# A hybrid decoder block on one core: attention regrouped into rounds of four steps, with half-height score matmuls, half-width value matmuls and a combination by features

## The chip, the core and the metric

The kernel runs on one core of one Trainium2 chip. The core has a matmul engine (PE; its weight loads are listed apart as PEld), a vector engine (DVE), an activation engine (ACT), a general engine (POOL), a queue that issues most transfers (SP), and 16 DMA engines that all transfers share. The metric is device time in microseconds (us) of one execution; several executions are timed and the median is taken.

## What is computed

One decoder block over a sequence of 2048 positions of 1024 features, in float32. One input projection feeds two branches: attention (branch A) and a gated recurrence (branch B); their gated outputs are projected, merged, projected again and normalised. The change concerns branch A:

```python
DILATION_GROUPS = ((128, 1), (512, 4), (2048, 16))     # (window, dilation); 8 heads of 64 in each group
# per group: positions regrouped by residue modulo the dilation, blocks of 128 queries,
# keys = [previous block, current block], causal band of width window // dilation
s = jnp.einsum('brnqhd,brnkhd->brnhqk', qb, kw) * (Dh ** -0.5)
s = jnp.where(valid, s, NEG_INF)
m = jnp.max(s, -1); p = jnp.exp(s - m); l = jnp.sum(p, -1)
o = jnp.einsum('brnhqk,brnkhd->brnqhd', p, vw) / l
lse = m + jnp.log(l)
# over the groups, per head slot and position:
attn = sum_g softmax_g(lse_g) * o_g
attn = attn * silu(g_attn);  y_a = attn @ w_attn_proj
```

## The kernel before, in words

The program is one hand-written order of instructions for each engine. `now["n"]` counts ticks; `later(lag, fn)` puts `fn`'s instructions into the streams `lag` ticks on, and `pe_later` does the same for a place inside PE's stream. An engine executes its own stream strictly in that order, and SP issues its transfers in that order too: a transfer whose buffer is not free yet holds up those written behind it.

Four stages follow one another. (1) The input projection, seven-multiplication products of 512-column matmuls (line L598), with all elementwise work of both branches beside it; queries go to DRAM as a rounded part and a rest (`qh_scr`, `ql_scr`, both pre-scaled), keys as they are (`k_scr`), values transposed (`v_scr`). (2) Attention. (3) The recurrent branch's projection `yb` (L1198 to L1200), with the combination of the three groups beside it. (4) The attention projection `ya`, the output projection and the normalisation.

**Attention before.** There are 12 units: a unit is one dilation group g and one pair of heads `hp` (`unit(u)`, in the order of groups 0, 2, 1). A unit has 16 steps, one for each block of 128 queries, so there are 192 steps. A step has two key blocks of 128 where there is a previous block ("full", 108 steps), and one otherwise ("half": all 64 of group 2, four of each unit of group 1, one of each unit of group 0, together 84).

- `step_s` computes scores. Heads have 64 features, and the 128 rows of a matmul hold two things at once: `A` stacks the query's rounded part above its rest, `B1` (tile B) holds the key's rounded part twice, and `b2` (tile C) the key's rest above zeros. Two matmuls for each head, accumulated in one bank (L973), give the three products that float32 accuracy needs. DVE adds the mask and takes the row's extreme (`tensor_tensor_reduce`, L977, and a small read of its accumulator); ACT takes the exponential (L979).
- `step_t` transposes the probabilities on PE (L988, two for each head) and ACT or DVE brings them from PSUM to SBUF (L993, L995).
- `step_v` multiplies: the transposed probabilities `ptb` are the stationary operand, V the moving one with 65 columns, of which one is all ones and gives the denominator (L1012; each of these float32 matmuls is two instructions on PE). DVE copies two steps' outputs out (L1016), and ACT issues their transfer to `o_scr` (L1026), 132 floats for each position: values, denominators, extremes.

PE's stream takes turns: the scores of step m, the transposes of step m-3, the values of step m-4. A unit's operands are loaded one unit ahead by `unit_parts` (six transfers: L784, L805); POOL rounds and splits the keys (L792, L793, L795), three passes over each half of the rows. V is loaded for two units at a time (`v_parts`, L822 to L826). The slots X0 to X5 hold the projection's inputs until its last products have read them, so the first unit's loads wait for those.

**Combination before** (`combine`, 16 calls of 512 positions by one head pair): three loads of `o_scr` by position (positions on partitions), 17 small DVE operations and one exponential for the weights (L1114 to L1131), three POOL multiplications and two additions of 128x512 (L1133 to L1135), four PE transposes to features (L1140), and the gate on DVE (L1145).

Of the kernel before, what the change touches and what calls it, by code (L numbers as in the profile page):

```python
# [8 lines left out]
F32 = mybir.dt.float32  # L9
# [6 lines left out]
P = 128  # L16
# [15 lines left out]
def hybrid_block_kernel(ctx: ExitStack, tc: tile.TileContext, a: dict, out: bass.AP):  # L32
# [10 lines left out]
    o_scr = [[dram.tile([S, 132], F32, name=f"o_scr{g}{hp}") for hp in range(HP)] for g in range(3)]  # L43
# [5 lines left out]
    v_scr = [[dram.tile([S, 260], F32, name=f"v_scr{g}{j}") for j in range(2)] for g in range(3)]  # L49
# [286 lines left out]
    vs_free = [sl_p.tile([P, 4, 130], F32, name=f"vs{j}") for j in range(2)]  # L336
    for t in vs_free:
        dve.memset(t[:, :, 0:1], 1.0)
        dve.memset(t[:, :, 129:130], 1.0)
    tog = {"n": 0}  # L340

    def v_chain(vt, sgn, f, c):
# [14 lines left out]
        act.activation(vs[:, :, 1:129], st["tp"], AF.Copy, scale=sgn)  # L357
        tog["n"] -= 1
        yield Ask()
        dst = v_scr[g][hp // 2][c * CH:(c + 1) * CH, (hp % 2) * 130:(hp % 2) * 130 + 130]  # L360
# [395 lines left out]
    lo_, up_ = slice(0, 64), slice(64, P)  # L756
    USLOT = (("X4", "X3", "X2"), ("Y0", "X1", "X0"))
    VSLOT = {(0, 0): "X5", (2, 0): "Y1", (1, 0): "Y2", (0, 1): "X5", (2, 1): "Y1", (1, 1): "Y2"}
    zero = [False, False]
    B2 = {}  # L760
# [7 lines left out]
    def unit_parts(u):  # L768

        sl = USLOT[u % 2]  # L770
        g, hp = unit(u)
        q = {n: qk_scr[n, 4 * g + hp] for n in ("qh", "ql", "k")}

        def k_part(h, hs, os):
            def fn():
                if h == 0:
                    units[u] = [None, big(sl[1], [P, 2, S], F32R, f"B{u}")]
                    if u < 2:
                        B2[u] = big(sl[2], [P, 2, S], F32R, f"C{u}")
                        pool.memset(flat(B2[u][up_, 0]), 0.0)  # L780
                        pool.memset(flat(B2[u][lo_, 1]), 0.0)
                    units[u].append(B2[u % 2])
                _, B1, b2 = units[u]
                sp.dma_start(flat(b2[hs, h]), q["k"][hs])  # L784

                def split(t):
                    if (u, h) == (0, 0):
                        act.activation(B1[hs, h, t], flat(b2[hs, h, t]), AF.Copy)
                        act.activation(B1[os, h, t], flat(B1[hs, h, t]), AF.Copy)
                        eng = dve  # L790
                    else:
                        pool.tensor_copy(B1[hs, h, t], flat(b2[hs, h, t]))  # L792
                        pool.tensor_copy(B1[os, h, t], flat(B1[hs, h, t]))  # L793
                        eng = pool
                    eng.tensor_tensor(out=b2[hs, h, t], in0=flat(b2[hs, h, t]), in1=flat(B1[hs, h, t]), op=ALU.subtract)  # L795

                later(3, lambda: split(slice(0, S // 2)))
                later(4, lambda: split(slice(S // 2, S)))
            return fn

        def q_part(hs, h, n, qs):
            def fn():
                if (hs, h) == (lo_, 0):
                    units[u][0] = big(sl[0], [P, 2, S], F32R, f"A{u}")
                sp.dma_start(flat(units[u][0][hs, h]), q[n][qs])  # L805
            return fn

        return [k_part(0, lo_, up_), k_part(1, up_, lo_), q_part(lo_, 0, "qh", lo_), q_part(up_, 0, "ql", lo_),
                q_part(lo_, 1, "ql", up_), q_part(up_, 1, "qh", up_)]

    VT = {}

    def v_parts(g, j):
        src = v_scr[g][j]

        def part(i):
            def fn():
                if i == 0:
                    VT[g, j] = big(VSLOT[g, j], [P, 16, 260], F32, f"V{g}{j}")
# [82 lines left out]
    first, second, firstv = unit_parts(0), unit_parts(1), v_parts(0, 0)  # L902
    low = NS
    where = [(s, j) for s in range(NQ) for j in range(ticks[s])]
    for T, (s, j) in enumerate(where):
# [10 lines left out]
        if s == NQ - 1:  # L916
            for fn in ((), (), first[:2], first[2:], firstv, second[:1], second[1:2])[j]:
                fn()
# [32 lines left out]
    def step_s(m):  # L951
        u, n = divmod(m, 16)
        g, _ = unit(u)
        A, B1, b2 = units[u]
        pv = prev(g, n)
        lo = 0 if pv is not None else P
        s = aps.tile([P, 2, 256], F32, tag="s", name=f"s{m}", bufs=3)
        if n % 4 == 0:
            st["osb"] = at_p.tile([P, 4, 132], F32, tag="osb", name=f"osb{m}", bufs=6)
        osb = st["osb"]  # L960
        for h in range(2):
            q = A[:, h, n * P:(n + 1) * P]
            for i, B in enumerate((B1, b2)):
                if g == 2:
                    k = B[:, h].rearrange("p (c r i) -> p r c i", c=4, r=16)[:, max(n - 1, 0):n + 1]
                elif pv is None:
                    k = B[:, h, n * P:(n + 1) * P]
                elif g == 0:
                    k = B[:, h, (n - 1) * P:(n + 1) * P]
                else:  # L970
                    c, r = divmod(n, 4)
                    k = B[:, h, (c - 1) * CH:(c + 1) * CH].rearrange("p (c r j) -> p r c j", c=2, r=4)[:, r]
                pe.matmul(s[:, h, (0 if g == 2 and n else lo):256], q, k, start=(i == 0), stop=(i == 1))  # L973
        p = at_p.tile([P, 2, 256], F32, tag="p", name=f"p{m}", bufs=5)
        for h in range(2):
            mm = osb[:, n % 4, 130 + h:131 + h]
            dve.tensor_tensor_reduce(out=p[:, h, lo:256], in0=s[:, h, lo:256], in1=mask[:, lo:256],  # L977
                                     scale=1.0, scalar=3e38, op0=ALU.add, op1=ALU.min, accum_out=mm)
            act.activation(p[:, h, lo:256], p[:, h, lo:256], AF.Exp, scale=-1.0, bias=mm)  # L979
        st["p", m] = (p, lo, osb)  # L980

    def step_t(m):
        p, lo, osb = st["p", m]
        pt = aps.tile([P, 4, P], F32, tag="t", name=f"pt{m}", bufs=3)
        ptb = at_p.tile([P, 4, P], F32, tag="pt", name=f"ptb{m}", bufs=3)
        for h in range(2):
            for x in range(lo // P, 2):
                pe.transpose(pt[:, 2 * h + x, :], p[:, h, x * P:(x + 1) * P], ident)  # L988
        dst, src = ptb, pt
        if lo:  # L990
            dst, src = (t.rearrange("p (h x) f -> p h x f", x=2)[:, :, 1, :] for t in (ptb, pt))
        if m % 3 == 1 or m % 3 and not 176 <= m < 187:
            act.activation(dst, src, AF.Copy)  # L993
        else:
            dve.tensor_copy(dst, src)  # L995
        st["t", m] = ptb

    def step_v(m):
        u, n = divmod(m, 16)
        g, hp = unit(u)  # L1000
        V = VT[g, hp // 2]
        vo = 130 * (hp % 2)
        p, lo, osb = st.pop(("p", m))
        ptb = st.pop(("t", m))
        if n % 2 == 0:
            st["o"] = aps.tile([P, 2, 130], F32, tag="o", name=f"o{m}", bufs=2)
        o = st["o"]
        pv = prev(g, n)
# [5 lines left out]
        if n % 2:  # L1014
            b = n % 4 - 1
            dve.tensor_copy(osb[:, b:b + 2, 0:130], o)  # L1016
# [40 lines left out]
    for fn in second[2:] + v_parts(2, 0):  # L1057
        fn()
# [373 lines left out]
```

## Time and profile before

| | |
|---|---|
| median of 3 runs | 2269.23 us (2264.55 to 2273.71) |
| span of the profiled execution | 2268.7 us, first to last instruction; no other time is given for it |
| PE / weight loads / DVE / ACT / POOL busy | 98% / 82% / 77% / 48% / 39% of the span |
| projection, until 1480 us | L598, over half of PE's instructions |
| attention, 1480 to 1814 us | 334 us |
| `yb` and combination, 1814 to about 1998 us | 32 jobs of 24 matmuls |
| the rest, to the end | `ya`, output projection, normalisation |

The table is read by stages: a busy share over the whole span says little of one stage. "PE busy" counts a matmul from its start to a modelled end, and consecutive matmuls overlap, so the distance from one start to the next (the pitch) is what a matmul costs where PE works without a pause.

### The profile page before, as it was taken

The numbers are of one execution on the slowest core, as the hardware profiler recorded it, in microseconds if no ns is written. First come the engines' busy times: TensorE is split into PE (matmuls) and PEld (weight loads), VectorE is DVE, ScalarE is ACT, GpSimd is POOL, SyncE is SP. The second block draws the span as 40 slices with busy tenths as digits, with TensorE's granted clock in tenths as the row PEclk, the third lists the DMA queues.
The fourth block names the chain that finished last, engine by engine and source line by source line (L and its number), as shares of the span: only waits on it lengthen the run. The fifth ranks groups of instructions, "written<-read, shape, count | busy, mean of one in ns | idle before, by whom it ended". The sixth has DMA issues, their size and how long they took to land.

```text
span 2268.7 us, 34220 instructions
## 1 busy us (share of the span) xinstructions
PE 2213.9 (98%) x11032; PEld 1868.7 (82%) x11032; DVE 1752.4 (77%) x3234; ACT 1091.3 (48%) x1982; POOL 874.6 (39%) x640
## 2 busy tenths in 40 slices
PE   7999999999999999999999999989999999999998
PEld 6888878888787788888888888878999888788887
DVE  8788878999898877778778878655666668967777
ACT  5344545456455656556566566555666621121010
POOL 1545544555454022222222212257676426722220
PEclk9999999999999999999999999999999999999999
DMA  7998897988987777686888787897786679884441
GB/s 227 268 259 254 244 266 222 273 267 269 273 266 249 258 215 225 201 241 208 252 276 258 249 250 237 251 256 176 206 217 160 191 234 316 287 271 167 130 140 65
DMA packets 327954, 526.01 MB, mean 232 GB/s; under 512 B 97120, under 2 KB 138080, under 8 KB 322912
## 3 DMA queue, kind: packets, MB, share of 16 engines
q1 hardware_dynamic: 297008, 479.05, 68.1%
q0 software_dynamic: 10080, 18.35, 5.1%
q10 hardware_dynamic: 20688, 26.42, 3.7%
q8 instruction: 88, 1.44, 0.3%
q14 instruction: 90, 0.74, 0.1%
HBM read 318.38 MB, written 190.64 MB: 224 GB/s over the span
## 4 chain that ended last, share of the span: by engine, by line
PE 57%; DMA 6%; DVE 2%; ACT 1%; POOL 1%; issue 1%; SPq 1%; ACTq 0%; DVEq 0%; POOLq 0%
PE q L598 29%; PE o L1012 4%; PE s L973 3%; PE z L1304 2%; PE z L1305 2%; PE z L1303 2%; PE yb L1198 2%; PE yb L1200 2%; PE yb L1199 2%; PE pt L988 2%; DMA A<-qh_scr 2%; PE ya L1271 1%; PE ya L1272 1%; PE ya L1270 1%; DMA l<-wl_scr 1%
## 5 line engine op out<-in xcount | busy, mean ns | idle before, releaser
L598 PE MATMUL q<-xT,hS 128*128 128x512 f32 x1680 | 520.9, 391 | 7.2 <-ACT e L621 6.0
L598 PE MATMUL q<-xT,l 128*128 128x512 f32 x1120 | 437.1, 390 | 0.0
L598 PE MATMUL q<-xB,hA 128*128 128x512 f32 x1248 | 389.7, 394 | 10.1 <-ACT xB L202 5.7
L598 PEld LDWEIGHTS q<-xT,hS 128*128 128x128 f32 x1680 | 314.9, 188 | 73.0 <-ACT e L621 6.4
L598 PE MATMUL q<-xB,l 128*128 128x512 f32 x904 | 354.6, 392 | 1.4 <-DMA l<-wl_scr 1.3
L598 PEld LDWEIGHTS q<-xB,hA 128*128 128x128 f32 x1248 | 234.7, 189 | 61.0 <-ACT xB L202 5.7
L598 PEld LDWEIGHTS q<-xT,l 128*128 128x128 f32 x1120 | 210.7, 188 | 44.1
L979 ACT ACTIVATE p<-p,osb 128x256 f32<-128x256 f32 (+1 forms) x384 | 156.2, 454 | 118.4 <-DVE osb L977 117.7
L214 POOL TENSOR_TENSOR S<-S,wA 128x512 f32<-128x512 f32 x35 | 45.7, 1306 | 422.6 <-DVE S L214 251.7
L977 DVE CUSTOM_DVE_ANT_0 p<-s,mask 128x256 f32<-128x256 f32 (+1 forms) x384 | 125.2, 364 | 103.0 <-PE s L973 61.5
L598 PEld LDWEIGHTS q<-xB,l 128*128 128x128 f32 x904 | 171.0, 189 | 38.5 <-DMA l<-wl_scr 2.2
L214 POOL TENSOR_TENSOR sw<-sw,sin 128x512 f32<-128x512 f32 x96 | 161.8, 1691 | 70.3 <-DMA sw<-y 64.6
L259 ACT ACTIVATE hA<-wA 128x512 fp32r<-128x512 f32 x218 | 135.5, 624 | 89.6 <-DMA wA<-in_w_in_dram 52.7
L598 PE MATMUL q<-xB,hS 128*128 128x512 f32 x560 | 174.9, 394 | 3.0 <-DVE v L214 3.0
L598 PE MATMUL q<-xT,hA 128*128 128x512 f32 x560 | 173.1, 390 | 3.1 <-ACT hi L323 1.8
L1012 PE MATMUL o<-V,ptb 128*128 128x65 f32 x1200 | 166.4, 277 | 8.0 <-ACT ptb L993 5.3
L1012 PEld LDWEIGHTS o<-V,ptb 128*128 128x128 f32 x1200 | 153.3, 196 | 19.4 <-ACT ptb L993 16.2
L259 ACT ACTIVATE hS<-S 128x512 fp32r<-128x512 f32 x175 | 109.2, 624 | 97.1 <-DVE S L214 51.3
L214 POOL TENSOR_TENSOR l<-wA,hA 128x512 fp32r<-128x512 f32 x68 | 105.2, 1547 | 80.3 <-ACT hA L259 61.6
L973 PE MATMUL s<-B,A 128*128 128x256 f32 (+1 forms) x384 | 116.8, 326 | 10.0 <-DMA A<-qh_scr 6.4
L598 PEld LDWEIGHTS q<-xT,hA 128*128 128x128 f32 x560 | 104.6, 188 | 26.6 <-issue 3.7
L598 PEld LDWEIGHTS q<-xB,hS 128*128 128x128 f32 x560 | 104.7, 189 | 25.1 <-issue 4.1
(196 smaller groups left out, 4853.0 us busy)
## 6 DMA issues: line engine op xcount, KB each, us to landing
wA<-in_w_in_dram SPq DMA_DIRECT2D x253, 256.0 KB, 5.0
wl_scr<-l SPq DMA_DIRECT2D x105, 512.0 KB, 5.3
l<-wl_scr SPq DMA_DIRECT2D x105, 512.0 KB, 4.7
sw<-y SPq DMA_DIRECT2D x384, 64.0 KB, 3.3
wS<-in_w_in_dram SPq DMA_DIRECT2D x70, 256.0 KB, 4.7
wS<-in_w_in_dram POOLq DMA_DIRECT2D x70, 256.0 KB, 6.6
o_scr<-osb ACTq DMA_DIRECT2D x48, 264.0 KB, 5.9
oc<-o_scr SPq DMA_DIRECT2D x48, 264.0 KB, 5.0
```

Source lines behind the costliest of these rows:

```text
L214: eng.tensor_tensor(out=out, in0=in0, in1=in1, op=op)
L259: act.activation(h, r, AF.Copy)
L598: pe.matmul(bank, w[:, ks], x[:, kk, xx], start=(first and i == 0), stop=(last and i == 11))
L973: pe.matmul(s[:, h, (0 if g == 2 and n else lo):256], q, k, start=(i == 0), stop=(i == 1))
L977: dve.tensor_tensor_reduce(out=p[:, h, lo:256], in0=s[:, h, lo:256], in1=mask[:, lo:256], scale=1.0, scalar=3e38, op0=ALU.add, op1=ALU.min ...
L979: act.activation(p[:, h, lo:256], p[:, h, lo:256], AF.Exp, scale=-1.0, bias=mm)
L988: pe.transpose(pt[:, 2 * h + x, :], p[:, h, x * P:(x + 1) * P], ident)
L1012: pe.matmul(o[:, n % 2, h * 65:h * 65 + 65], ptb[:, 2 * h + x, :], V[:, kb, vo + h * 65:vo + h * 65 + 65], start=(x == lo // P), stop=(x = ...
L1198: pe.matmul(yb, WL[f][:, 0, k], xx[:, 0], start=(k == 0), stop=False)
L1199: pe.matmul(yb, WL[f][:, 0, k], xx[:, 1], start=False, stop=False)
L1200: pe.matmul(yb, WL[f][:, 1, k], xx[:, 0], start=False, stop=(k == 7))
L1303: pe.matmul(z, mh[:, k], w[:, 0, hs], start=(k == 0), stop=False)
```

## The change

**Rounds.** The loop runs over 48 rounds of four steps. In round i PE gets three phases: all 24 score matmuls of round i, the transposes of round i-1, the values of round i-1.

**Scores.** A unit's operands are now plain: tile A is [features of both heads, rounded part or rest, 2048], tile B the same for the keys. Each of the three products is a matmul over 64 rows, and the two heads of a pair, on rows 0 to 63 and 64 to 127, are issued in turn and write different banks: six matmuls for each step where there were four. Group 2 and first blocks use 128 columns of keys (group 2 streamed 256 before, and used 128).

**Values.** V is now the stationary operand with 64 columns, `ptb` the moving one with 128; head 0 writes partitions 0 to 63 of the output, head 1 partitions 64 to 127. The output is thus [features, queries]. The column of ones is gone: ACT's exponential accumulates the denominator itself (`accum_out`). `leave` copies four steps at once (512 columns) and puts positions back into their order; SP issues the transfers, extremes and denominators go to `st_scr` in rows of 16 bytes.

**Loads.** Unit operands are loaded two units ahead into three pairs of slots, in four transfers; the keys' split is two passes instead of three, over all 128 rows at once, in quarters of 512 columns. The first unit's loads are written one tick earlier, and unit 2's come ahead of the loop.

**Combination.** All weights are computed once (`weigh`), transposed four times (`spread`), and spread over features by a matmul with a 0/1 matrix (three of 512 columns for each `combine`); DVE multiplies each group's values by them, POOL adds twice and multiplies by the gate.

```diff
@@ attention, cut to its core
-        s = aps.tile([P, 2, 256], F32, tag="s", name=f"s{m}", bufs=3)
...
-                pe.matmul(s[:, h, (0 if g == 2 and n else lo):256], q, k, start=(i == 0), stop=(i == 1))
+        for w in range(2):
+            s = st["s", i, w] = [aps.tile([P, 2, 256], F32, tag="s", name=f"s{i}{w}{h}", bufs=4) for h in range(2)]
+            for j in range(2):
...
+                for x, y in ((0, 0), (1, 0), (0, 1)):
+                    for h, hs in enumerate(HALF):
+                        K = B[hs, y]
...
+                        pe.matmul(s[h][:, j, lo:256], A[hs, x, n * P:(n + 1) * P], k, start=(x + y == 0), stop=(y == 1))
...
-            act.activation(p[:, h, lo:256], p[:, h, lo:256], AF.Exp, scale=-1.0, bias=mm)
+        act.activation(p, p, AF.Exp, scale=-1.0, bias=s[:, h:h + 1], accum_out=s[:, 2 + h:3 + h])
...
-                pe.matmul(o[:, n % 2, h * 65:h * 65 + 65], ptb[:, 2 * h + x, :], V[:, kb, vo + h * 65:vo + h * 65 + 65],
-                          start=(x == lo // P), stop=(x == 1))
+                    v0 = P * (hp % 2) + 64 * h
+                    pe.matmul(o[hs, j, :], V[:, n if x else prev(g, n), v0:v0 + 64], ptb[:, 2 * h + x, :],
+                              start=(x == first(i, j) // P), stop=(x == 1))
@@ the loop
+    for i in range(NG + 2):
...
+        if on:
+            scores(i)
+        if i > 1:
+            leave(i - 2)
+        if off:
+            expo(i - 1, 3, 0)
+            expo(i - 1, 3, 1)
+        if on:
+            peak(i, 0, 0)
+            peak(i, 0, 1)
+            expo(i, 0, 0)
+            peak(i, 1, 0)
+        if off:
+            turn(i - 1, 0)
+            bring(i - 1, 0, act)
+            turn(i - 1, 1)
+            bring(i - 1, 1, dve)
...
+            turn(i - 1, 2)
+            bring(i - 1, 2, act)
...
+            turn(i - 1, 3)
+            bring(i - 1, 3, act if i % 2 and u % 3 != 1 else dve)
+            values(i - 1)
...
@@ loads and combination
-    USLOT = (("X4", "X3", "X2"), ("Y0", "X1", "X0"))
+    USLOT = (("X3", "X2"), ("X0", "X4"), ("Y0", "X1"))
...
+                bc = fp.tile([P, CH], F32, tag="z", name=f"bc{nm}{g}", bufs=3)
+                pe.matmul(bc, W["sel"][:, 3 * hp + g].rearrange("p h d -> p (h d)"), W[c], start=True, stop=True)
+                dve.tensor_tensor(out=oc[:, g], in0=oc[:, g], in1=bc, op=ALU.mult)
+            for g in (1, 2):
+                pool.tensor_tensor(out=oc[:, 0], in0=oc[:, 0], in1=oc[:, g], op=ALU.add)
+            pool.tensor_tensor(out=oc[:, 3], in0=oc[:, 0], in1=oc[:, 3], op=ALU.mult)
```

How the streams move is shown at three places. In these rows a name is the tile with the number of its buffer, the line is that of the kernel in question, and `x4` counts like instructions in a row.

PE, before, in the first unit: one step's scores (two of its four), the transposes and values that stand behind them, and the next step's first scores.

```order
L973 MATMUL s_14605<-B_14239,A_14262 128x256
L973 MATMUL s_14605<-C_14240,A_14262 128x256
...
L988 MATMUL pt_14616<-ident,p_14542 128x128 x4
L1012 MATMUL o_14623<-V_14282,ptb_14594 128x65 x4
L973 MATMUL s_14629<-B_14239,A_14262 128x256
```

PE, after, in the same unit: the end of a round. The scores' four tiles (two of a round's four banks are shown first), then the four steps' transposes, then their values, then the next round.

```order
L973 MATMUL s_14421<-B_14215,A_14239 128x256
L973 MATMUL s_14422<-B_14215,A_14239 128x256
...
L973 MATMUL s_14435<-B_14215,A_14239 128x256
L973 MATMUL s_14436<-B_14215,A_14239 128x256
...
L995 MATMUL pt_14462<-ident,p_14396 128x128 x4
L995 MATMUL pt_14473<-ident,p_14400 128x128 x4
L995 MATMUL pt_14481<-ident,p_14404 128x128 x4
L1018 MATMUL o_14488<-ptb_14467,V_14281 64x128 x4
L1018 MATMUL o_14488<-ptb_14478,V_14281 64x128 x4
L1018 MATMUL o_14488<-ptb_14486,V_14281 64x128 x4
L973 MATMUL s_14512<-B_14215,A_14239 128x256
```

The kind of matmul changed three times in a step before, and changes three times in a round of four steps now; the stationary operand of the scores alternates between the two heads.

ACT, before: two exponentials for each step, a bring for two steps of three, and the transfer of the outputs.

```order
L979 ACTIVATE p_14611<-p_14611,osb_14606 128x256 x2
L1026 DMA o_scr_58<-osb_14424 128x4x132
L979 ACTIVATE p_14634<-p_14634,osb_14606 128x256 x2
L993 ACTIVATE ptb_14640<-pt_14639 128x512
L979 ACTIVATE p_14656<-p_14656,osb_14606 128x256 x2
L993 ACTIVATE ptb_14662<-pt_14661 128x512
L979 ACTIVATE p_14678<-p_14678,osb_14606 128x256 x2
```

ACT, after, one round: exponentials and brings are woven, each exponential also writes the denominator (`sta`), and the last two of a round come at the start of the next.

```order
L988 ACTIVATE p_15555,sta_15416<-p_15555,sta_15416 128x256
L1003 ACTIVATE ptb_15564<-pt_15561 128x2x128
L988 ACTIVATE p_15555,sta_15416<-p_15555,sta_15416 128x256
L1003 ACTIVATE ptb_15582<-pt_15577 128x512
L988 ACTIVATE p_15559,sta_15416<-p_15559,sta_15416 128x256
L1003 ACTIVATE ptb_15590<-pt_15585 128x512
L988 ACTIVATE p_15559,sta_15416<-p_15559,sta_15416 128x256
L988 ACTIVATE p_15575,sta_15416<-p_15575,sta_15416 128x256 x2
L988 ACTIVATE p_15608,sta_15416<-p_15608,sta_15416 128x256 x2
```

The transfer left ACT's stream; eight exponentials and two or three brings stand in a round.

SP, before, where attention's operands are first loaded: keys and queries of unit 0 in six transfers, then V, then unit 1.

```order
L784 DMA C_14240<-k_scr_82 64x2048 x2
L805 DMA A_14262<-qh_scr_80 64x2048
L805 DMA A_14262<-ql_scr_81 64x2048 x2
L805 DMA A_14262<-qh_scr_80 64x2048
L822 DMA V_14282<-v_scr_74 128x4x260 x4
L784 DMA C_14311<-k_scr_106 64x2048 x2
```

SP, after, at the same place.

```order
L787 DMA B_14215<-k_scr_83 128x1024 x2
L797 DMA A_14239<-qh_scr_81 128x2048
L797 DMA A_14239<-ql_scr_82 128x2048
L787 DMA B_14259<-k_scr_107 128x1024 x2
L813 DMA V_14281<-v_scr_75 128x4x256 x4
L797 DMA A_14307<-qh_scr_105 128x2048
L797 DMA A_14307<-ql_scr_106 128x2048
```

Unit 1's keys now stand ahead of V, and the same bytes of a unit go in four transfers over all rows.

More of the change, by code (lines that the diff above doesn't have):

```diff
@@ L982, in step_t @@
[L982 to L992, printed above, removed]
+        return 0 if prev(g, 4 * q + j) is not None else P
@@ L1154, in prep_wa @@
+        pe_later(1, mix)
     def prep_wa(f, lag):
```

364 lines of the change are left out of this document (204 added, 160 removed).

## The prediction

> **What bounds the kernel now.** I read the stages first, as shares over the whole span hide them. Columns: window, its length, busy time of each engine, granted clock, share of the DMA engines' time, GB/s.
>
> ```profile
> core 0: us, PE busy (x) PEld busy (x) DVE busy (x) ACT busy (x) POOL busy (x), PEclk, DMA share, GB/s
> 1480.00:1814.00 334.00, 313.95 (x2567) 301.97 (x2566) 201.03 (x937) 211.86 (x523) 209.62 (x144) 0.96 0.76 200
> 1814.00:1990.00 176.00, 174.20 (x798) 143.68 (x798) 142.85 (x368) 31.85 (x69) 96.30 (x80) 1.00 0.86 279
> ```
>
> Attention is the first row: 334 us, PE 94% busy and its weight loads 90%, DVE and ACT near 60%. So PE bounds it, and inside PE something that goes with the number of weight loads. Projection before it and output stages after it are untouched except by the combination (second row). The timeline of PE in a full step says what a step costs (start, length, what):
>
> ```profile
> 1641.25 1.00 PE L1012 MATMUL o<-V,ptb 128*128 128x65 f32 x8
> 1642.06 0.36 PE L973 MATMUL s<-B,A 128*128 128x256 f32 x1
> 1642.26 0.28 PE L973 MATMUL s<-C,A 128*128 128x256 f32 x1
> 1642.38 0.28 PE L973 MATMUL s<-B,A 128*128 128x256 f32 x1
> 1642.50 0.28 PE L973 MATMUL s<-C,A 128*128 128x256 f32 x1
> 1642.62 0.60 PE L988 MATMUL pt<-ident,p 128*128 128x128 f32 x4
> 1643.05 1.09 PE L1012 MATMUL o<-V,ptb 128*128 128x65 f32 x8
> ```
>
> Starts matter, not lengths. Scores take 1642.06 to 1642.62, 0.56 us, at a pitch of 0.12; four transposes 0.43 (0.107 each); eight value instructions 0.81 to 0.90 (0.10 to 0.11 each, although only 65 columns stream). A full step is thus 1.80 to 1.90, say 1.83. Half steps, from the values of one to those of the third after it:
>
> ```profile
> 1613.27 0.66 PE L1012 MATMUL o<-V,ptb 128*128 128x65 f32 x4
> 1617.12 0.66 PE L1012 MATMUL o<-V,ptb 128*128 128x65 f32 x4
> ```
>
> 3.85 for three, 1.28 each. 108 full and 84 half steps make 198 + 108 = 306 us; the other 28 of 334 are waits, mostly in the first units:
>
> ```profile
> 1464.26 1.14 SPq L784 DMA_DIRECT2D C<-k_scr  x2
> ```
>
> ```profile
> PE s L973 <- DMA A<-qh_scr: 6.4, 2, 3.5
> ```
>
> ```profile
> 1512.21 0.33 PE L973 MATMUL s<-B,A 128*128 128x128 f32 x1 [3.57 <-POOL B L793]
> 1517.91 0.41 PE L973 MATMUL s<-B,A 128*128 128x256 f32 x1
> 1518.12 0.41 PE L973 MATMUL s<-C,A 128*128 128x256 f32 x1
> ```
>
> The first row is SP's timeline, the second the list of waits (us in total, times, longest), the rest PE's timeline. The first loads go out at 1464; PE then waits for queries (6.4 us), and from 1508 for POOL's split of unit 1's keys. After that wait its pitch is 0.21 instead of 0.12 for some microseconds: a long pause costs the clock too.
>
> **The change, part by part.** A round replaces four steps. Of the 48 rounds, 28 are full; 20 are half (16 of group 2, the first of each group-1 unit).
>
> *Scores on PE.* 24 matmuls of 64 rows for 16 of 128. Nothing in the trace shows matmuls on halves of the array. Floor: the two heads run side by side, 12 pairs at the row's 0.12, 1.44 us a round. Ceiling: one after another, 24 x 0.12 = 2.88. Half rounds use 128 columns, whose pitch the start of attention shows:
>
> ```profile
> 1483.60 0.30 PE L973 MATMUL s<-B,A 128*128 128x128 f32 x1 [2.88 <-DMA A<-qh_scr]
> 1483.73 0.29 PE L973 MATMUL s<-C,A 128*128 128x128 f32 x1
> ```
>
> 0.13, so no cheaper than 256: 1.56 to 3.12. I take the floor: the operands lie on disjoint rows and the outputs in different banks, so nothing that I see in the program ties the two together.
>
> [...]
>
> *Transposes.* Unchanged in number: 16 x 0.107 = 1.71 a round (half: 0.86).
>
> *Values on PE.* 32 instructions in a full round as before (16 in a half one), now with 64 stationary columns and 128 moving ones. Floor: pairs side by side, 16 x 0.11 = 1.76. Ceiling: 3.52, as before (half 0.88 to 1.76). I take the floor for the same reason: disjoint output partitions. PE sums to 1.44 + 1.71 + 1.76 = 4.91 in a full round (before 4 x 1.83 = 7.32) and 1.56 + 0.86 + 0.88 = 3.30 in a half one (before 5.12).
>
> *The mode changes.* Bounded from rows: today's change from values to scores costs 0.08 (first score pitch 0.20 against 0.12); a full drain would be about the 0.28 that a lone matmul lasts. 0.24 to 0.84 a round; with the former PE is at 5.15.
>
> *ACT.* Now PE is no longer far ahead of the others, so their rows count, by group (busy us, mean ns of one, idle before):
>
> ```profile
> L979 ACT ACTIVATE p<-p,osb 128x256 f32<-128x256 f32 x216 | 97.9, 501 | 62.3 <-DVE osb L977 62.2
> L993 ACT ACTIVATE ptb<-pt 128x512 f32<-128x512 f32 x70 | 40.3, 576 | 2.4 <-PE pt L988 2.4
> L993 ACT ACTIVATE ptb<-pt 128x256 f32<-128x256 f32 x54 | 19.5, 361 | 0.0
> L977 DVE DVE_READ_ACCUMULATOR2_ANT osb<- 128x1 f32 x384 | 31.9, 83 | 0.0
> L1118 ACT ACTIVATE cE<-cE 128x24 f32<-128x24 f32 x16 | 3.6, 224 | 130.8 <-DVE cE L1117 130.8
> ```
>
> and in time:
>
> ```profile
> 1488.93 0.91 ACT L979 ACTIVATE p<-p,osb 128x256 f32<-128x256 f32 x2
> 1489.74 0.57 ACT L993 ACTIVATE ptb<-pt 128x512 f32<-128x512 f32 x1
> 1528.57 0.69 ACT L979 ACTIVATE p<-p,osb 128x128 f32<-128x128 f32 x2 [0.19 <-DVE osb L977]
> 1529.17 0.36 ACT L993 ACTIVATE ptb<-pt 128x256 f32<-128x256 f32 x1
> ```
>
> A pair of exponentials occupies ACT until the next instruction starts: 0.81, so 0.405 each, and 0.30 each for 128 columns. The accumulated denominator is new on ACT. Bounds: nothing, or a small activation's 0.224 (L1118). I take the 0.083 that DVE's read of its accumulator takes, the nearest in kind. Full round: 8 x (0.405 + 0.083) + 2.5 x 0.576 = 5.34. Half: 8 x (0.30 + 0.083) + 2 x 0.361 = 3.79. ACT is therefore the longest of the three, just above PE. ACT's issue of the output transfers leaves, to SP, behind loads that have two units' time.
>
> *DVE.*
>
> ```profile
> L977 DVE CUSTOM_DVE_ANT_0 p<-s,mask 128x256 f32<-128x256 f32 x216 | 83.0, 422 | 51.6 <-PE s L973 28.4 <-ACT ptb L993 18.0 <-ACT p L979 2.5
> L995 DVE COPY ptb<-pt 128x512 f32<-128x512 f32 x38 | 26.1, 686 | 0.0
> ```
>
> Eight peaks of at most 0.42, 1.5 brings and one output copy of 0.69: 5.1 at most, under ACT.
>
> *Stalls by order.* In a round ACT still has five exponentials (2.4 us) after its last bring; meanwhile PE finishes the values (the last step's quarter, 0.44), runs half the scores (0.72) and DVE takes the first peak (0.42): 1.6 us, so ACT's next exponential is ready in time. Handovers of PE, DVE and ACT that are not covered: I add 0.3 us a round, 14 us, three times the 0.1 between a peak and its exponential today.
>
> *Loads.* Full-speed stretches of the DMA engines give the rate:
>
> ```profile
> 1612.00:1640.00 28.00, 26.92 (x222) 25.06 (x222) 18.42 (x99) 19.59 (x55) 19.51 (x13) 1.00 0.99 259
> ```
>
> The first three units and their V are 3 x 3.15 + 3 x 2.1 = 15.7 MB, with two units' outputs 17.8 MB, 69 us at 259 GB/s from 1464: 1533. At the speeds above, unit 2's values begin at 1480 + 4 x 5.6 + 4 x 4.1 + 4 = 1523. So 10 us of waiting. POOL's split, which made PE wait, falls to two passes, and unit 1's keys come ahead of V: its 3.6 us goes. Over the whole stage the same 67 MB (334 us x 200 GB/s) at 259 take 258 us: after the change the transfers are almost as long as the work, which is why I don't let the stage shrink below that.
>
> *Sum for attention.* 28 x 5.34 + 16 x 3.79 + 4 x 4.0 = 226; + 14 handovers + 6 to fill and drain (scores ahead, transposes and values behind: 1.4 + 3.5, and latency) + 10 loads = 256 us, for 334: **-78 us**.
>
> *Combination.* It runs beside `yb`, where PE is 99% busy, so PE's balance counts. Pitch of 512-column matmuls there:
>
> ```profile
> 1923.63 0.39 PE L1200 MATMUL yb<-h,wl 128*128 128x512 f32 x1
> 1924.31 0.39 PE L1200 MATMUL yb<-h,wl 128*128 128x512 f32 x1
> ```
>
> Three starts in 0.68: 0.227. Added: 48 x 0.227 + 16 transposes x 0.107 = 12.6; removed: 64 x 0.107 = 6.8. **+6 us.** POOL's five operations become three and DVE's 17 small ones three of 512 columns; neither is on the path, since DVE has 33 us to spare in that window. `weigh` waits for the last unit's statistics on DVE, behind which `yb`'s drains queue; four banks (some 20 us of PE) cover that. The start of `yb` needs eight splits that POOL now does alone in the last four rounds: **+2 us**, an estimate from a 1.28 us subtraction each:
>
> ```profile
> L1035 POOL TENSOR_TENSOR h<-h 128x512 fp32r<-128x512 f32 x8 | 10.2, 1279 | 19.4 <-ACT h L1034 19.4
> ```
>
> Together -78 + 6 + 2 = -70. The profiled span is 2268.7, half a microsecond under the median of 2269.23, so both give 2199; I say **2200**.
>
> **The rivals.**
>
> (a) *Pairs run one after another.* For it: no row shows halves working together. PE is then 2.88 + 1.71 + 3.52 = 8.11 in a full round and 3.12 + 0.86 + 1.76 = 5.74 in a half one, 342 us, with 16 for loads and ends 358: +24, +8 elsewhere, **2300**, slower. It decides once a full round takes PE longer than today's 7.32 us: pairing must save a tenth of the serial 8.11 to break even.
>
> (b) *Only one of the two kinds pairs up,* or the matmuls pair and the loads don't. Scores serial, values paired: 2.88 + 1.71 + 1.76 = 6.35 and 4.86; 275 + 16 = 291: **2234**. Values serial: 6.67 and 4.18, 270 + 16: **2229**. For it: the weight-load rows are 90% busy, and 24 loads replace 16.
>
> [...]
>
> (c) *The denominators are dear on ACT.* At 0.224 each, 8 x 0.141 = 1.13 more in each of 48 rounds: +54, **2254**. Against it: DVE's 0.083.
>
> (d) *Transfers bound.* The 258 us above at a rate of 240 would be 279: **2222**.
>
> **How the numbers follow.** My case (ACT bounds, pairs overlap, 2180 to 2218) 0.50; (b), (c), (d) and full drains, 2218 to 2258, 0.35; around no change, as when two of these meet, 0.05; (a) 0.10. The range 2180 to 2258 leaves out the last two. Within 0.5% (11 us, about what a measurement can tell from no change) lie 2258 to 2281: faster 0.85, same 0.05, slower 0.10. With everything at its floor (no handovers, no load waits) it would be 2175.
>
> **What would show it.** Right: score starts of the two heads nearly coincide, 24 in about 1.5 us; values 32 in about 1.8; rounds of 5.3 to 5.8 us full and about 4 half; ACT over 85% busy in attention; attention ending near 1736; `yb` 6 us longer. Wrong: scores 0.12 apart one by one (a); ACT's exponentials over 0.5 apart (c); PE waiting on loads all through (d); a granted clock under 0.9, since PE would pause more often.

## The result, and the profile after

The changed kernel takes **2194.04 us** (median of 4 runs, 2193.32 to 2197.86) against 2267.76 for the kernel before in the same comparison: a ratio of 0.968 (95% interval 0.966 to 0.970). The forecast was 2200, with a range of 2180 to 2258. The profiled execution spans 2191.6 us where that of before spans 2268.7, so the two traces stand 77.1 us apart and can be compared stage by stage:

| stage | before, us | after, us | difference | forecast |
|---|---|---|---|---|
| projection | 1480.4 | 1483.9 | +3.5 | 0 |
| attention | 334.0 | 240.3 | -93.7 | -78 |
| `yb` and combination | 184.3 | 189.4 | +5.1 | +8 |
| `ya` to the end | 269.8 | 277.8 | +8.0 | 0 |

The total is right within 7 us, but attention gained 16 us more than forecast and two stages lost some 11 us that were not foreseen. The table of windows of the changed kernel (columns as in the forecast: window, its length, busy time of PE, weight loads, DVE, ACT and POOL, granted clock, DMA share, GB/s):

```profile
core 0: us, PE busy (x) PEld busy (x) DVE busy (x) ACT busy (x) POOL busy (x), PEclk, DMA share, GB/s
1483.88:1725.50 241.62, 235.13 (x2959) 202.87 (x2959) 192.15 (x902) 226.67 (x889) 95.74 (x104) 0.98 0.78 262
1484.00:1524.00 40.00, 38.88 (x478) 33.55 (x479) 30.38 (x154) 36.36 (x147) 20.08 (x23) 0.96 1.01 391
```

The first row is attention. PE went from 94% to 97% busy, and ACT from 63% to 94%: two engines are now close to their limit where one was. DVE stands at 80%. The second row is the first 40 us of it, where the loads of three units crowd: the DMA engines moved 391 GB/s there. PE's timeline shows the phases of a half round and of a full one (start, length, what, number of instructions):

```profile
1514.51 1.55 PE L973 MATMUL s<-B,A 64*128 64x128 f32 x24
1515.99 1.35 PE L995 MATMUL pt<-ident,p 128*128 128x128 f32 x8
1517.27 1.09 PE L1018 MATMUL o<-ptb,V 128*64 128x128 f32 x16
1518.30 1.55 PE L973 MATMUL s<-B,A 64*128 64x128 f32 x24
...
1609.70 1.70 PE L973 MATMUL s<-B,A 64*128 64x256 f32 x24
1611.33 2.00 PE L995 MATMUL pt<-ident,p 128*128 128x128 f32 x16
1613.26 1.97 PE L1018 MATMUL o<-ptb,V 128*64 128x128 f32 x32
1615.15 0.39 PE L973 MATMUL s<-B,A 64*128 64x256 f32 x2
```

As in the forecast the starts count. In the full round shown scores take 1.63 (1609.70 to 1611.33; 1.62 in most rounds), transposes 1.93, values 1.89 to 1.90: 5.45 us (1609.70 to 1615.15; other full rounds up to 5.56) for four steps that took 7.3 before. A half round is 3.79 (1514.51 to 1518.30): 1.48, 1.28 and 1.03. So 24 half-height score matmuls cost 0.0675 each where a full-height one cost 0.12: the two heads do run side by side. The list of PE's waits in attention (us in total, times, longest) is short, and no load is in it:

```profile
PE pt L995 <- ACT ptb L1003: 3.8, 2, 2.9
PE s L973 <- DVE sta L980: 0.9, 1, 0.9
PE o L1018 <- ACT ptb L1003: 0.8, 3, 0.3
```

The longest, 2.9 us, has its cause elsewhere: ACT's brings stand behind exponentials that wait for a peak, and DVE takes that peak only after it has split weights of `yb` (L1058), which themselves waited for ACT.

```profile
1700.22 2.19 DVE L1058 SCALAR_TENSOR_TENSOR wl<-wl 128x512 fp32r<-128x512 f32 x2 [1.10 <-ACT wl L1057]
1704.36 0.69 PE L995 MATMUL pt<-ident,p 128*128 128x128 f32 x2 [2.94 <-ACT ptb L1003]
```

The granted clock is 0.67 from 1700 to 1710, and by the lengths of the rounds this one place costs the stage about 5 us.

Behind attention, the group of `yb` matmuls (first and last start are in it) stretches from 1724.2 to 1912.8. `ya` follows at once, but PE has to wait 39 us into it; the chain that ended last and SP's list of waits (us in total, times, longest) show how that came about, in SP's queue (chain: start, length, what):

```profile
L1271 PE MATMUL yb<-h,wl x256: 389/389/497, 1724.2 to 1912.8; 128*128 128x512 f32 x128
```

```profile
1845.64 5.93 DMA at_scr<-oc
1851.63 0.32 SPq L1212
...
1944.77 7.13 DMA at<-at_scr
1952.01 0.64 ACT at L1054
```

```profile
SPq L1212 <- DMA at_scr<-oc: 41.1, 14, 4.7
```

The load of a combination's operands (L1212, into `oc`) stands on SP until the previous but one has left the buffer: the transfer `at_scr<-oc` of 5.93 us ends at 1851.57 and SP goes on at 1851.63. Everything else that SP issues queues behind it; SP spends 41.1 us in 14 such waits. PE's own wait is at the end of that, one of 3.81 us:

```profile
1952.69 0.79 PE L1349 MATMUL ya<-at,wa 128*128 128x512 f32 x1 [3.81 <-ACT at L1054]
```

### The profile page after: what moved, and what is told of

It is laid out like the page before. It is cut to its first block, busy times and chain, and to the rows that moved or that the text cites. A ratio compares the mean times of both kernels' runs of the same rounds, so it can differ in the third digit from the quotient of the medians.

```text
span 2191.6 us, 34893 instructions
## 1 busy us (share of the span) xinstructions
PE 2152.8 (98%) x11416; PEld 1773.0 (81%) x11416; DVE 1704.5 (78%) x2972; ACT 1105.1 (50%) x2336; POOL 727.2 (33%) x565
## 4 chain that ended last, share of the span: by engine, by line
PE 82%; DMA 9%; DVE 3%; SPq 2%; issue 1%; ACT 1%; POOL 0%; ACTq 0%; DVEq 0%; POOLq 0%
PE q L596 59%; DMA at_scr<-oc 4%; PE s L973 3%; PE pt L995 3%; PE o L1018 3%; PE z L1382 2%; PE z L1384 2%; PE z L1383 2%; PE ya L1349 1%; PE ya L1350 1%; PE ya L1351 1%; PE vtp L347 1%; DMA ybr<-yb_scr 1%; PE g L466 1%; PE g L468 1%
## 5 line engine op out<-in xcount | busy, mean ns | idle before, releaser
L596 PEld LDWEIGHTS q<-xB,l 128*128 128x128 f32 x904 | 170.3, 188 | 41.1 <-DVE l L215 0.5
L988 ACT ACTIVATE p<-p,sta 128x256 f32<-128x256 f32 (+1 forms) x384 | 172.5, 455 | 7.9 <-DVE sta L980 7.3
L980 DVE CUSTOM_DVE_ANT_0 p<-s,mask 128x256 f32<-128x256 f32 (+1 forms) x384 | 119.1, 361 | 8.0 <-PE s L973 3.6
L215 DVE TENSOR_TENSOR y<-y,cos 128x512 f32<-128x512 f32 x96 | 104.8, 1097 | 15.8 <-DMA sw<-y 15.7
L1355 POOL TENSOR_TENSOR me<-gA,ybr 128x512 f32<-128x512 f32 x32 | 51.8, 1632 | 184.2 <-DVE gA L1354 165.7
L1384 PE MATMUL z<-wo,ml 128*128 128x512 f32 (+1 forms) x264 | 101.1, 383 | 0.8 <-DVE ml L1368 0.8
```

The lines of the kernel that those rows point to most:

```text
L215: eng.tensor_tensor(out=out, in0=in0, in1=in1, op=op)
L596: pe.matmul(bank, w[:, ks], x[:, kk, xx], start=(first and i == 0), stop=(last and i == 11))
L980: dve.tensor_tensor_reduce(out=st["p", i, j][:, h, lo:256], in0=st["s", i, j // 2][h][:, j % 2, lo:256], in1=mask[:, lo:256], scale=1.0, s ...
L988: act.activation(p, p, AF.Exp, scale=-1.0, bias=s[:, h:h + 1], accum_out=s[:, 2 + h:3 + h])
L1355: pool.tensor_tensor(out=ME[c][:, f], in0=ga, in1=yb, op=ALU.add)
L1384: pe.matmul(z, ml[:, k], w[:, 0, hs], start=False, stop=(k == 7))
```

## The experiments

Ten kernels were run. All ratios are against the kernel before; the changed kernel stands at 0.968. Where a phase is named, its length is from one phase's start to the next one's.

**Do the score pairs need the two heads in turn?** The order of six matmuls of a step becomes three of head 0, then three of head 1.

```diff
-                for x, y in ((0, 0), (1, 0), (0, 1)):
-                    for h, hs in enumerate(HALF):
+                for h, hs in enumerate(HALF):
+                    for x, y in ((0, 0), (1, 0), (0, 1)):
```

> The changed kernel with the score matmuls of a step in another order: three of head 0, then three of head 1, instead of the heads in turn. Same instructions. Theory (pairs on disjoint rows run side by side): a score phase of 24 goes from 1.62 us towards 24 x 0.12 = 2.9 us (at least 2.3, since the third of one head can still overlap the first of the other), PE is the longest engine of a round, so 0.7 to 1.3 us in each of 48 rounds: 33 to 60 us more, 2225 to 2255. Rival (the phase is short for another reason, as cheaper loads of half height; order is no matter): 2194, within 0.5%.

Measured: 2197.16 us, ratio 0.967 (0.966 to 0.969). PE's timeline:

```profile
1607.07 1.69 PE L973 MATMUL s<-B,A 64*128 64x256 f32 x24
1608.70 1.75 PE L995 MATMUL pt<-ident,p 128*128 128x128 f32 x14
```

The phase is 1.63 us, as in the changed kernel. The run therefore did not take the pairing away, and says nothing yet on what pairing is worth: three matmuls of one half in a row still find their partners.

**Longer runs on one half.** Six of head 0 then six of head 1 in each pair of steps; then twelve and twelve in a round; then both heads on rows 0 to 63, so that no partner is left (the scores of head 1 are then those of head 0).

```diff
@@ six
             for h, hs in enumerate(HALF):
                 for j in range(2):
                     ...
                     for x, y in ((0, 0), (1, 0), (0, 1)):
@@ twelve
         for h, hs in enumerate(HALF):
             for w in range(2):
                 for j in range(2):
                     ...
@@ one half
-                    for h, hs in enumerate(HALF):
+                    for h, hs in enumerate((HALF[0], HALF[0])):
```

> The changed kernel with six score matmuls of head 0 (two steps), then six of head 1, twice in a round. Three with three paired fully (phase 1.62), twelve with twelve hardly (2.68 in place of 3.07 on one half, 0.4 saved at one change of head, so some three matmuls overlap at a change). Theory (a fixed look-ahead of about three matmuls): three changes of head in a phase save 3 x 0.4 of 3.07, phase about 1.9 to 2.1, 48 x 0.35 = 17 us more, 2205 to 2218. Rival (the look-ahead is long, and twelve failed for the waits on the banks at its end): 1.62 and 2194.

> The changed kernel with all twelve score matmuls of head 0 of a round first, then the twelve of head 1 (peaks of head 1 thus start later). Theory A with a short look-ahead: twelve of a kind can't pair, phase 2.6 to 2.9 us as with one half, and DVE's peaks of head 1 wait; 2245 to 2270. Theory A with a look-ahead of over twelve matmuls, or B: phase near 1.62, time near 2200 (a little more, from the later peaks).

> The changed kernel with both heads' score matmuls on rows 0 to 63 (head 0's operands for both, so head 1's scores are left out). Same number and shape of instructions, but no partner on other rows. Since the order of heads within a step made no difference, two theories are left. Theory A (pairs side by side, and the engine looks far enough ahead to pair three with three): a phase of 24 goes from 1.62 to 24 x 0.107 to 0.12, 2.6 to 2.9 us; 48 x 1.1 = 53 us more, about 2247. Theory B (a matmul of 64 rows is twice as fast by itself): phase 1.62, time 2194.

Measured: six 2209.68 us, 0.975 (0.971 to 0.978); twelve 2239.27 us, 0.987 (0.982 to 0.991); one half 2286.99 us, 1.009 (1.006 to 1.011), slower than before. Score phases of full rounds in PE's timelines of the three, in this order:

```profile
1566.55 2.03 PE L973 MATMUL s<-B,A 64*128 64x256 f32 x24
1568.51 2.06 PE L995 MATMUL pt<-ident,p 128*128 128x128 f32 x16
```

```profile
1606.99 2.74 PE L975 MATMUL s<-B,A 64*128 64x256 f32 x24
1609.67 2.00 PE L997 MATMUL pt<-ident,p 128*128 128x128 f32 x16
```

```profile
1530.54 5.38 PE L973 MATMUL s<-B,A 64*128 64x128 f32 x24
1535.85 1.97 PE L995 MATMUL pt<-ident,p 128*128 128x128 f32 x8
...
1554.59 3.14 PE L973 MATMUL s<-B,A 64*128 64x256 f32 x24
1557.66 2.00 PE L995 MATMUL pt<-ident,p 128*128 128x128 f32 x16
...
1602.47 2.89 PE L973 MATMUL s<-B,A 64*128 64x128 f32 x24
1605.29 1.41 PE L995 MATMUL pt<-ident,p 128*128 128x128 f32 x8
```

The same 24 matmuls take 1.62 us in runs of one or three, 1.96 in runs of six, 2.68 in runs of twelve and 3.07 without a partner. Runs of one and of three take the same; against them runs of six lose 0.34 us and runs of twelve 1.06. Pairing thus saves 1.45 us in a full round (3.07 less 1.62) and 1.34 in a half one (2.82 less 1.48): 28 x 1.45 + 20 x 1.34 = 67 us of the attention stage. This was rival (b) with the scores serial, which the forecast put at 2234. By these 67 us alone the change would have kept some 7 of the 74 us that it gains; that the run ended slower than the kernel before has a second reason, which follows.

The weight loads show the pairing itself. Within the first 0.1 us of a score phase (windows 1514.50:1514.60 and 1607.65:1607.75) two loads start in the changed kernel, and one in the run with one half:

```profile
1514.51 0.19 PEld L973 LDWEIGHTS s<-B,A 64*128 64x128 f32 x2 [0.17 <-issue]
```

```profile
1607.65 0.18 PEld L973 LDWEIGHTS s<-B,A 64*128 64x128 f32 x1 [0.17 <-issue]
```

The half-round phase at 1530.54 lasts 5.31 us, the one at 1602.47, of the same 24 matmuls, 2.82. The windows say why: PE's granted clock fell to 0.53 for some 20 us while PE was busy without a gap.

```profile
1530.00:1550.00 20.00, 20.00 (x112) 18.11 (x109) 7.31 (x39) 8.85 (x42) 7.35 (x8) 0.53 0.43 159
1553.00:1600.00 47.00, 46.72 (x480) 42.50 (x479) 29.78 (x129) 36.60 (x131) 7.41 (x8) 1.00 0.35 104
1530.00:1817.00 287.00, 285.06 (x2556) 256.51 (x2552) 165.84 (x772) 199.37 (x768) 73.79 (x80) 0.88 0.52 166
```

The third row is nearly all of attention: 0.88 there on average. So of the 93 us that this kernel lost against the changed one, 67 are the pairing; the other 26 are about what the clock makes, by an estimate (0.12 of 287 us is 34 us, less the 2% that the changed kernel loses too: 29).

Without a partner a half-height load and its matmul cost 0.118 to 0.128 each (2.82 and 3.07 us for 24), about what a full-height one cost in the kernel before (0.12 to 0.13). With the heads in turn the loads of the two halves overlap, and a load with its matmul costs 0.0675.

**The value pairs.** All value matmuls of head 0, then all of head 1.

```diff
-        for j in range(4):
...
-            for x in range(first(i, j) // P, 2):
-                for h, hs in enumerate(HALF):
+        for h, hs in enumerate(HALF):
+            for j in range(4):
...
+                for x in range(first(i, j) // P, 2):
```

> The changed kernel with the value matmuls of a round in another order: all of head 0, then all of head 1. Same instructions. Theory (pairs on disjoint columns run side by side): a value phase of 32 goes from 1.90 us to about 3.4 (32 x 0.107), a half one from 1.03 to 1.7; 28 x 1.5 + 20 x 0.7 = 56 us more, about 2250. Rival (the gain is that a load of 64 columns costs half of one of 128): no change, 2194 within 0.5%.

Measured: 2242.63 us, 0.987 (0.986 to 0.989).

```profile
1617.40 3.33 PE L1018 MATMUL o<-ptb,V 128*64 128x128 f32 x32
1620.66 1.70 PE L973 MATMUL s<-B,A 64*128 64x256 f32 x24
```

The phase takes 3.26 us for 1.90, and 1.67 for 1.02 in half rounds: 28 x 1.36 + 20 x 0.65 = 51 us, and the run lost 49. In the profiled executions attention alone is 47 us longer.

Where the gain comes from is another question than what pairing is worth. Four full steps of the kernel before spent 4 x 0.56 = 2.24 us on scores and 4 x 0.81 to 4 x 0.90, 3.2 to 3.6 us, on values. Against these a full round saves 0.6 us on scores and 1.3 to 1.7 on values: the pairing of the scores mostly pays for their greater number, and the values bring most of the gain.

**Mode changes.** Twelve phases a round for three: six scores, four transposes, eight values, four times; the values run one step behind.

```diff
+            scores_step(i, 0)
+            values_step(i - 2, 3)
...
+            turn(i - 1, 0)
...
+            scores_step(i, 1)
+            turn(i - 1, 1)
...
+            values_step(i - 1, 0)
```

> The changed kernel with PE's three phases of a round cut into twelve: six scores, four transposes, eight values, four times over; values one step behind their transposes, the output copy moved behind them, ACT and DVE in the same order but for that. Theory (a change of kind costs about 0.2 us, as the phases' lengths show: 1.62 for 1.44, 1.93 for 1.71, 1.90 for 1.71): nine more changes a round, 1.8 us, 48 x 1.8 = 86 us more, about 2280, so no gain over the kernel before. Rival (changes are free, the phases only spread waits): within 1% of 2194.

Measured: 2258.79 us, 0.995 (0.993 to 0.996): 65 us slower than the changed kernel. Its window of attention, and its weight loads in time:

```profile
1484.00:1780.00 296.00, 291.19 (x2894) 204.85 (x2894) 194.71 (x895) 226.12 (x874) 94.38 (x103) 0.99 0.65 216
```

```profile
1601.30 0.41 PEld L979 LDWEIGHTS s<-B,A 64*128 64x128 f32 x6 [0.17 <-issue]
```

PE is busy 291 of 296 us, so the time is not in waits for other engines. The weight loads pause 0.17 us where the kind changes from values to scores (the bracket), with nothing that the profile shows to wait for. 65 us over 48 x 9 additional changes are 0.15 us each, and 61 of the 65 lie in attention. By this price, as an estimate, three changes a round cost the changed kernel 0.45 to 0.5 us each round, 22 to 24 us in all.

So a change of kind has a price here, 0.15 to 0.17 us; the 0.28 that the forecast took for a full drain was its author's estimate, and no run shows it.

**Does ACT bind?** The accumulation of denominators is left out; they are set to 1.

```diff
-        act.activation(p, p, AF.Exp, scale=-1.0, bias=s[:, h:h + 1], accum_out=s[:, 2 + h:3 + h])
+        act.activation(p, p, AF.Exp, scale=-1.0, bias=s[:, h:h + 1])
```

> The changed kernel without the accumulated denominators: ACT's exponentials write none, the denominators are set to 1 (left out of the result). ACT has 8 x 0.09 us less in a round. Theory (full rounds of 5.45 us are bound by PE: 1.62 + 1.93 + 1.90; half rounds of 3.79 by ACT: 8 x 0.39 + 0.7): full rounds keep their length, half ones fall to PE's 3.4: 20 x 0.35 = 7 us less, 2187. Rival (ACT bounds all rounds, as the prediction's sum had it): 48 x 0.72 = 35 us less, 2160.

Measured: 2193.43 us, 0.966 (0.964 to 0.967), no different from the changed kernel. ACT's rows in the changed kernel, and this run's window and half rounds:

```profile
1604.24 0.51 ACT L988 ACTIVATE p<-p,sta 128x256 f32<-128x256 f32 x1
1604.66 0.19 ACT L988 ACTIVATION_READ_ACCUMULATOR p<-p,sta 128x1 f32 x1
1604.75 0.49 ACT L988 ACTIVATE p<-p,sta 128x256 f32<-128x256 f32 x1
```

```profile
1484.00:1721.00 237.00, 231.76 (x2945) 200.61 (x2945) 190.62 (x900) 196.12 (x504) 96.32 (x115) 0.99 0.82 268
```

```profile
1572.60 1.55 PE L974 MATMUL s<-B,A 64*128 64x128 f32 x24
...
1574.99 0.20 PEld L996 LDWEIGHTS pt<-ident,p 128*128 128x128 f32 x2 [0.28 <-ACT ptb L1004]
...
1576.39 0.89 PE L974 MATMUL s<-B,A 64*128 64x128 f32 x12
```

An exponential with its denominator costs ACT 0.51 (1604.24 to 1604.75) or 0.49, not the sum of the two rows: the read of the accumulator lasts 0.19 but adds only some 0.095 to the 0.405 of an exponential alone. Without it ACT is busy 196 us instead of 227, and a half round still takes 3.79, where 3.4 had been expected. What is left there is not ACT's load: the fourth step's transposes need the first of three banks back and wait 0.28 us for ACT's bring (the bracket), and ACT itself stands idle for 0.24 us before that bring, waiting for PE. PE and its hand-over to ACT and back set the rounds; ACT's work stands just under them.

**Loads one unit ahead.** The changed kernel's rounds, with the look-ahead of the loads cut back by one unit.

```diff
-        if i % 4 == 0 and 1 <= u <= 9:
-            loads += unit_parts(u + 2)
+        if i % 4 == 0 and 1 <= u <= 10:
+            loads += unit_parts(u + 1)
-    for fn in v_parts(2, 0) + third:
+    for fn in v_parts(2, 0):
```

> The changed kernel with unit operands loaded one unit ahead, as before the change, instead of two (unit 2's no longer before the loop). Theory (the waits of the first units, some 28 us in the kernel before, were one of two sources of the gain; with work of 3.8 us rounds a unit of group 2 gives only 15 us for 3.15 MB, its split and V): PE waits of 3 to 5 us at the unit behind each group-2 unit and 5 to 10 at the start, 15 to 25 us more, 2210 to 2220. Rival (loads are hidden either way): 2194 within 0.5%.

Measured: 2234.18 us, 0.985 (0.981 to 0.988): +40 us, more than either theory gave. PE's timeline at three units' starts, and the window:

```profile
1590.86 0.47 PE L973 MATMUL s<-B,A 64*128 64x128 f32 x2 [8.98 <-DMA A<-qh_scr]
...
1622.77 0.48 PE L973 MATMUL s<-B,A 64*128 64x128 f32 x2 [7.14 <-DMA A<-qh_scr]
...
1656.25 0.91 PE L973 MATMUL s<-B,A 64*128 64x128 f32 x4 [6.70 <-POOL B L780]
```

```profile
1560.00:1762.00 202.00, 169.51 (x2044) 146.21 (x2042) 132.33 (x623) 157.41 (x619) 68.34 (x73) 0.89 0.68 208
```

The groups take turns from unit to unit, and these are the starts of one unit each of groups 1, 0 and 2. PE stands 23 us before them in these rows alone, 32 us in the whole window, and the granted clock is 0.89 in the window that holds the pauses. Work behind a pause is slow too: after the one of 8.98 us the eight transposes of a half round take 1.89 us (1595.78 to 1597.67), where those ahead of it took 1.27 (1579.51 to 1580.78). The two-unit look-ahead is a part of the change in its own right, worth 40 us with rounds this short.

**The late `ya`.** Three buffers for the combination's operands instead of two.

```diff
-    cb_p = stC.enter_context(tc.tile_pool(name="cb_p", bufs=2, reuse_waits="tile"))
+    cb_p = stC.enter_context(tc.tile_pool(name="cb_p", bufs=3, reuse_waits="tile"))
```

> The changed kernel with three buffers instead of two for the combination's operands. The chain of after runs through at_scr<-oc for 4% of the span: SP must not overwrite a buffer before the result in it has been written out, and all loads behind that wait. Theory (this delay is why the start of the attention projection loses 5 us to late loads, PE waiting 3.8 us on L1349): 4 to 6 us less, 2189. Rival (those loads are late because the transfers themselves are saturated at 300 GB/s there): no change, within 1 us.

Measured: 2186.70 us, 0.964 (0.961 to 0.966). This is the fastest complete version, 7.3 us under the changed kernel by the medians; the two intervals just touch. The same stretch of both kernels, from the end of `yb` to the end, first the changed one:

```profile
1913.60:2191.60 278.00, 264.48 (x1177) 217.97 (x1175) 192.73 (x325) 36.41 (x60) 51.80 (x32) 0.99 0.45 151
```

```profile
1913.90:2183.60 269.70, 261.58 (x1177) 217.26 (x1175) 187.92 (x318) 32.89 (x55) 52.49 (x32) 0.99 0.43 144
```

278.0 becomes 269.7, the length that the stage had before (269.8): the loss behind `yb` was this buffer wait. SP's waits of L1212 for `at_scr<-oc` and PE's wait in `ya` are gone from the lists.

**The price of the combination on PE.** On the version with three buffers, the matmuls that spread the weights are left out, and a fourth plane of the same buffer stands in for them.

```diff
-                bc = fp.tile([P, CH], F32, tag="z", name=f"bc{nm}{g}", bufs=3)
-                pe.matmul(bc, W["sel"][:, 3 * hp + g].rearrange("p h d -> p (h d)"), W[c], start=True, stop=True)
-                dve.tensor_tensor(out=oc[:, g], in0=oc[:, g], in1=bc, op=ALU.mult)
+                dve.tensor_tensor(out=oc[:, g], in0=oc[:, g], in1=oc[:, 3], op=ALU.mult)
```

> The kernel with three mix buffers (2186.7 us) without the spreading matmuls: the groups' values are multiplied by the gate instead of by the weights spread by a matmul (the weighting is left out). DVE does the same number of operations, from SBUF. Theory (PE bounds this stage, so 48 x 0.227 = 11 us of matmuls are paid in full): 2176. Rival (they fit into gaps of PE beside the loads): no change, within 2 us of 2186.7.

Measured: 2179.60 us, 0.962 (0.959 to 0.964), 7 us under its base.

```profile
L1269 PE MATMUL yb<-h,wl x256: 389/389/497, 1723.1 to 1899.9; 128*128 128x512 f32 x128
```

```profile
PE ya L1347 <- ACT at L1054: 2.5, 1, 2.5
```

`yb` runs from 1723.1 to 1899.9, 176.8 us; with the matmuls and three buffers it was 187.8. So the 48 matmuls cost the 48 x 0.227 = 10.9 that the forecast gave them. The stage behind is some 5 us longer than in its base (275.0 for 269.7): PE now waits 2.5 us in `ya` for the combination's results, which is where part of the saving went.

## Why the prediction held, and where it did not

- **Pairs side by side: right.** The floors taken were 1.44 for scores and 1.76 for values; measured 1.62 and 1.90, each with a change of kind of about 0.17 in it, which leaves 1.45 and 1.73. The reason given, disjoint rows and disjoint partitions, is what the runs with one half and with separate heads bear out: 67 and about 50 us. Scores of half rounds were put at 1.56; less a change they took 1.31.
- **Mode changes: mis-sized.** The sum used the low end, 0.24 a round; it is near 0.5, in the middle of the bounds. With 3 x 0.17 PE's sum of 4.91 becomes 5.42, and 5.45 was measured. In half rounds 0.28 us more goes on the wait for ACT's first bring.
- **"ACT is therefore the longest of the three": wrong.** The terms were close (0.50 measured for an exponential with its denominator, 0.488 forecast), but PE's sum was short by the mode changes, and so ACT appeared to be ahead. The run without denominators shows that PE sets the round. That the full round came out near its 5.34, and the half one at its 3.79, is luck: two engines with almost the same sum.
- **Handovers, fill and load waits: mis-sized.** The rounds alone were forecast at 226 us and took about 28 x 5.45 + 16 x 3.79 + 4 x 4.43 = 231 (4.43 where a unit of group 1 begins). To this the forecast added 30 us; the stage of 240.3 leaves 9, of which 5 are the place at 1700 us. PE is without work for 6.5 us of the window, and its clock there is 0.98. The 10 us for loads did not occur: the rate of 259 GB/s, read from a stretch at 0.99 DMA share, was no ceiling, since 391 GB/s were moved in the first 40 us. For the same reason the 258 us that the stage was not to fall below were no floor; the forecast's own sum of 256 was already under it. The run with loads one unit ahead shows that the term is real where the look-ahead is shorter.
- **Combination and start of `yb`: right together.** +8 forecast, +5.1 measured; the matmuls alone cost 10.9 as worked out. The 2 us at the start of `yb` are not seen apart.
- **Behind `yb`: missing.** No step of the forecast looked at the combination's two buffers. Loads that waited for a buffer, 41.1 us in 14 waits, held the whole of SP's queue; 8 us came back as a late `ya`.
- **The projection's +3.5 us** lies before attention, where PE's matmuls are the same in both kernels and in the same order. In the profiles of the ten experiments, whose projection is that of the changed kernel, attention starts between 1483.3 and 1488.7 us, so part of the 3.5 is spread; all of them are later than the one profile of the kernel before. No run was made on it, and its cause stays open.

The rivals: both sides of (b) were tried as kernels; pairs lost on one kind cost 45 to 49 us where the heads were separated, so the change would still have been faster than before by 1.3%. With scores confined to one half it is slower than before by 0.9%, values still paired and the lower clock included. (a), with both kinds serial, was not run; the two prices added to the stage, 240 + 67 + 51 = 358 us, are what (a) had worked out. (c) and (d) did not occur.

## What to carry to other kernels

Small matmuls on two halves of the array were worth pairing here, where their number and not their length set PE's time (0.13 us at 128 columns, 0.12 at 256, in the kernel before): a pair cost about what one full-height matmul did (0.135 us with its share of the changes, against 0.12), and short alternating runs (of one and of three here) sufficed. Group them by kind, since a change cost 0.15 to 0.17 us, more than a pair of matmuls. When a stage gets more than a quarter shorter, go through everything that it hid: here the second engine came within a few per cent of the first, a load ahead by one unit would have been late, and a pool of two buffers held up a queue two stages on.

## What had not been expected

With the score matmuls on rows 0 to 63 alone, the granted clock was 0.53 over 20 us in which PE was busy for all 20, and then 1.00 again with the same instructions. In the kernel before a low clock stood behind a pause: 0.66 from 1516 to 1521, behind waits of 3.57 and 2.08 us. Here no pause of PE stands ahead of it: from 1498.61 on each group in PE's timeline starts before the one ahead has ended. It came again in a later unit of group 2, where a score phase took 5.31 us (1694.64 to 1699.95), and not in the unit whose rounds run from 1602.47 to 1623.04, where they took 2.82 to 2.83. What sets the clock was not examined.

With a DMA share near 1, rates still differed: 391 GB/s in the first 40 us of attention, at a share of 1.01, and 259 in a stretch of the kernel before, at 0.99. The two stretches held different transfers; which difference between them sets the rate was not examined.
